# Block 0's gates by indirect accumulating DMAs into a zeroed table, in a hybrid decoder block on one Trainium2 core

## The chip, the cores and the metric

The kernel runs on one core of a Trainium2 chip, as one launch. The metric is the device time of that launch in microseconds (us). The core has five engines that work side by side, each with a queue of its own that it works off in order: TensorE (PE in the profile; its weight loads are the row PEld), VectorE (DVE), ScalarE (ACT), GpSimd (POOL) and SyncE (SP), which here issues the plain DMAs. Sixteen transfer engines move the data of all queues.

## The reference, cut to what matters

One decoder layer over 1024 tokens of width 1024. After a mixer (a gated DeltaNet and a sliding-window attention) comes PEER, a retrieval of single-neuron experts, and the change lies in it:

```
qry = (ht @ wq).reshape(T, 8, 2, 128)               # 8 heads, two half queries
sc = einsum("thpd,hpnd->thpn", qry, sub_keys)       # 128 scores per half
top_s, top_i = top_k(sc, 16)
cand = all sums of one score of each half           # 256 per head
best_s, best_pos = top_k(cand, 16)
expert = i1 * 128 + i2                              # of 16384 experts
gates = softmax(best_s)                             # 16 per head, 128 per token
act = gelu(x_token . u_tab[expert])
y_token = sum(gates * act * v_tab[expert])
```

A token so has 128 pairs (expert, gate). Within a head the 16 experts differ; two heads may pick the same expert, and then both gates count. After PEER come a gated projection and a last norm.

## The kernel before, in words

Tokens are handled in 8 blocks of 128. First comes the upstream part (`upstream`): the projections in two halves of 512 tokens (`project`, whose loop over 12 column tiles `ct` does the convolution), then, in four groups of two blocks, the mixers of the next group and the retrieval of this one (`retrieve`, which calls `topk` for each block). Weights and activations are split into two parts of type fp32r, so that one product becomes three matmuls (`mm3`, L141); other products are plain float32.

PEER's experts are evaluated in two ways. For blocks 5, 6 and 7 (`ABLK`), rows of the tables U and V are gathered by GpSimd, one indirect DMA of 128 rows for each of 128 pairs and each table, and VectorE multiplies and adds them (`gather_dots`, `gather_block`). For blocks 0 to 4 (`DBLK`, 640 tokens, `NU`) all 16384 experts are evaluated densely (`dense`, L924): in 128 chunks of 128 experts, U's product with the 640 tokens (in two `parts` of 320 columns, L938 to L940, 24 matmuls each), a gelu, a multiplication by the gates and a split into wh and wl; after each group of four chunks (`GC`) the product with V, 3 x 4 matmuls of 512 columns for each of 5 blocks and 2 halves.

The dense path needs the gates as a table over experts and tokens, with zeros where a token didn't pick an expert. `gbuild` (L837) makes it block by block: for four tokens at a time it compares a row of numbers with i1 and i2 (VectorE, tile `o12`, 128x1024), scales one of the two results by the gate (ScalarE, four times), multiplies the two on TensorE (float32, 128 columns, four products) and copies the result to `stage`; after 16 tokens `stage` goes to the DRAM table `gd` (1 MB). A block has 32 such steps and 8 writes. `dense` loads `gd` for a group of four chunks at a time into `Gt`, which has one buffer.

The order of the instructions of each engine is worked out ahead by a planner, from the order in which the program is written and a simulated time line; the calls `tick(us)` are in the program a count of VectorE work done, which a job may use to advance (before, none is there upstream). GpSimd does little upstream: the inverse roots of the norms and of the mixers (`rsqrt`, L154 to L157, tiles `rs_v`, `rs`, `rq`, `ro`) and small sets and copies.

Of the kernel before, what the change touches and what calls it, by code (L numbers as in the profile page):

```python
# [6 lines left out]

F32 = mybir.dt.float32
F32R = mybir.dt.float32r
# [9 lines left out]
P = 128  # L19
# [8 lines left out]
GROUPS = [[0, 1], [2, 3], [4, 5], [6, 7]]  # L28
HBLK = []
DBLK = [0, 1, 2, 3, 4]  # L30
ABLK = [5, 6, 7]
UBLK = HBLK + ABLK
BBLK = HBLK + DBLK
# [12 lines left out]
def _consts():  # L46
    import numpy as np

    r = np.arange(P)
    parts = [np.eye(P), r[:, None] <= r[None, :], r[:, None] > r[None, :], np.ones((P, P)),  # L50
             np.broadcast_to(r[None, :], (P, P)), r[None, :] > r[:, None]]
    for l in range(7):
        s = 1 << l
        same = (r[:, None] // (2 * s)) == (r[None, :] // (2 * s))
        low = same & (r[:, None] % (2 * s) >= s) & (r[None, :] % (2 * s) < s)
        parts.append(low if l == 0 else low.T[:, r % (2 * s) >= s])
    sel = np.zeros((P, 8 + 50 + 16 + 16 + 16))
    sel[:, :8] = (500000.0 ** (-np.arange(0, 16, 2) / 16)).astype(np.float32)
    widths = [16 // (a + 1) for a in range(16)]
    starts = np.concatenate([[0], np.cumsum(widths)[:-1]])  # L60
    sel[:, 58:74] = starts
    sel[:, 74:90] = np.concatenate([[0], np.diff(starts)])
    sel[:, 90:106] = np.arange(16)
    return np.concatenate([np.concatenate(parts, axis=1), sel], axis=1).astype(np.float32)
# [3 lines left out]
def block_kernel(ctx: ExitStack, tc, I, out, dbg=None):  # L68
# [6 lines left out]
    def copy(o, i, **k):  # L75
        return S.activation(o, i, AF.Copy, **k)  # L76

    def tt(o, a, b, op):
        return V.tensor_tensor(o, a, b, op)  # L79

    def stt(o, a, s, b, op0, op1, **k):
        return V.scalar_tensor_tensor(o, a, s, b, op0, op1, **k)  # L82

    def bc(ap, axis, n):
        u = ap.unsqueeze(axis)
        shape = list(u.shape)
        shape[axis] = n
        return u.to_broadcast(shape)
# [35 lines left out]
    UI, SL, ones = (C[n] for n in ("ui", "sl", "ones"))  # L124

    negt = c2.tile([P, 1], F32, name="negt")

    def load_consts():
        nc.sync.dma_start(ident, I["consts"][:, 0:P])
        nc.sync.dma_start(iota, I["consts"][:, 4 * P:5 * P])  # L130
        nc.sync.dma_start(cst, I["consts"][:, P:])
        V.tensor_copy(sel_b.rearrange("p s a h -> p (s a) h"), bc(sel[:, 58:106], 2, 8))
        V.memset(negt, NEG)

    def mm(o, l, r, start=True, stop=True):
        PE.matmul(o, l, r, start=start, stop=stop)  # L136
# [9 lines left out]
    x1d = dr.tile([NBLK, P, D], F32, name="x1d")  # L146
    h2d = dr.tile([len(UBLK), P, D], F32, name="h2d")
    h2Td = [dr.tile([P, DK, NU], F32, name=f"h2Td{i}") for i in range(2)]
    gd = dr.tile([NE // GC, P, NT // TB, GC, TB], F32, name="gd")

    eidx = cp.tile([P, len(UBLK), P], I32, name="eidx")
    gate_a = cp.tile([P, len(UBLK), P], F32, name="gate_a")

# [69 lines left out]
    def project(hf, es):  # L223
# [30 lines left out]
        for ct in range(12):  # L254
            wh, wl = weights(I["wc"][ct], [P, DK, P])
            if hf:
                for i in range(2 * ct, 2 * ct + 2):
                    cached_tile(i)
            raw = sm.tile([P, 3 + H], F32, tag="craw", name="craw")
            if hf:  # L260
                V.tensor_copy(raw[:, :3], prevs[:, ct])
            else:
                V.memset(raw[:, :3], 0.0)
            pc = bank("acc")
            for dk in range(DK):
                mm3(pc, wh[:, dk], wl[:, dk], hTh[:, dk], hTl[:, dk], dk == 0, dk == DK - 1)
            copy(raw[:, 3:], pc)
            if not hf:
                V.tensor_copy(prevs[:, ct], raw[:, H:H + 3])
            acc = sm.tile([P, H], F32, tag="cacc", name="cacc")  # L270
            copy(acc, raw[:, 3:], scale=convw[:, ct, 3:4])
            for j in (2, 1, 0):
                stt(acc, raw[:, j:j + H], convw[:, ct, j:j + 1], acc, ALU.mult, ALU.add)
            th = raw[:, 3:]
            S.activation(th, acc, AF.Tanh, scale=0.5)
            stt(acc, th, 1.0, acc, ALU.add, ALU.mult)
            qs = sm.tile([P, HB, P], F32, tag="cst", name="cst")
            pt = bank("tp", [HB, P])
            for i in range(HB):
                tr(pt[:, i, :], acc[:, i * P:(i + 1) * P])  # L280
            copy(qs, pt)
            nc.sync.dma_start(qkvn[b0:b0 + HB, :, ct, :].rearrange("b p c -> p b c"), qs)
# [474 lines left out]
    def topk(tk, bg, b, v, iu):  # L757
# [49 lines left out]
            summed(i2.rearrange("p (h k) -> p k h", h=8)[:, ks], t3)  # L807
            tick(7.5)

        ga = gate_a[:, UBLK.index(b)] if b in UBLK else flat[:, 2 * P:3 * P]  # L810
        gv = ga.rearrange("p (h k) -> p h k", k=16)
        tt(gv, bs, bs[:, :, 0:1].to_broadcast([P, 8, 16]), ALU.subtract)
        S.activation(gv, gv, AF.Exp)
# [3 lines left out]
        tt(gv, gv, bc(gs, 2, 16), ALU.mult)  # L817
        if b in UBLK:
            stt(eidx[:, UBLK.index(b)], i1, 128.0, i2, ALU.mult, ALU.add)
        if b in ABLK:  # L820
            return
        pt = bank("gm", [4, P])
        tr(pt[:, 0], i1)
# [9 lines left out]
            tick(1.4)  # L833

    slots = {}

    def gbuild(bg, b):  # L837
        tT = slots[b]
        for tb in range(P // TB):
            stage = bg.tile([P, NE, TB], F32, tag="stage", name="stage", bufs=2)  # L840
            for t0 in range(0, TB, 4):
                c0 = tb * TB + t0
                o12 = bg.tile([P, 2, 4, P], F32, tag="o12", name="o12", bufs=2)
                o1, o2 = o12[:, 0], o12[:, 1]
                tt(o12, bc(bc(iota, 1, 4), 1, 2), bc(tT[:, 0:2, c0:c0 + 4], 3, P), ALU.is_equal)
                for i in range(4):
                    copy(o2[:, i], o2[:, i], scale=tT[:, 2, c0 + i:c0 + i + 1])
                pg = bank("gm", [4, P])
                for i in range(4):
# [3 lines left out]
            nc.sync.dma_start(gd[:, :, BBLK.index(b) * (P // TB) + tb].rearrange("g p c t -> p g (c t)"),  # L853
                              stage.rearrange("p (g c) t -> p g (c t)", c=GC))

    def fetched(gp, tab, u, s):
# [59 lines left out]
        advance(1 << 20)  # L916

    def tick(us):
        credit[0] += us * RATE
        n = int(credit[0])  # L920
        credit[0] -= n
        advance(n)

    def dense(xB):  # L924
        with ExitStack() as es:
# [9 lines left out]
            for i in range(2):  # L935
                nc.sync.dma_start(hT[i].bitcast(F32), h2Td[i])
            nc.sync.dma_start(xB, x1d[BBLK[0]:BBLK[0] + NB].rearrange("b p d -> p b d"))
            nparts = (NU + 511) // 512  # L938
            width = (NU // nparts + TB - 1) // TB * TB
            parts = [(n0, min(width, NU - n0)) for n0 in range(0, NU, width)]  # L940
            total = len(ABLK) * 2 * P
            steps = NE + NE // GC * NB * 2
            count = [0, 0]
# [21 lines left out]

            nxt = prepared(0)
            for cg in range(NE // GC):
                Gt = ap.tile([P, NT // TB, GC, TB], F32, tag="Gt", name="Gt", bufs=1)
                nc.sync.dma_start(Gt, gd[cg])
                vs, ws = [], []  # L970
                for ci in range(GC):
                    c = cg * GC + ci
                    uh, ul, vh, vl = nxt
                    vs.append((vh, vl))
                    wh = ap.tile([P, NT], F32R, tag="wh", name="wh", bufs=GC + 1)
                    wl = ap.tile([P, NT], F32R, tag="wl", name="wl", bufs=GC + 1)
                    if NH:
                        gh = Gt[:, 0:NH // TB, ci, :]
                        sh = lambda x: x[:, 0:NH].rearrange("p (t k) -> p t k", k=TB)
                        copy(sh(wh), gh)  # L980
                        tt(sh(wl), gh, sh(wh), ALU.subtract)
                    for n0, n in parts:
                        pa = bank("u", [n])
                        for dk in range(DK):
                            mm3(pa, uh[:, dk], ul[:, dk], hT[0][:, dk, n0:n0 + n], hT[1][:, dk, n0:n0 + n],
                                dk == 0, dk == DK - 1)
                        ge = ap.tile([P, n], F32, tag="ge", name="ge")
                        S.activation(ge, pa, AF.Gelu_apprx_tanh)  # L988
                        g3 = ge.rearrange("p (t k) -> p t k", k=TB)
                        m0 = NH + n0  # L990
                        tt(g3, g3, Gt[:, m0 // TB:(m0 + n) // TB, ci, :], ALU.mult)
# [74 lines left out]
                post(*cur)  # L1066

    upstream()
    pools["gp"] = ctx.enter_context(tc.tile_pool(name="gp", bufs=GBUF, side="right", reuse_waits="tile"))
    pools["gx"] = ctx.enter_context(tc.tile_pool(name="gx", bufs=GXBUF, side="right", reuse_waits="tile"))  # L1070
    with tc.tile_pool(name="xB", bufs=1, side="right", reuse_waits="tile") as xp:
# [62 lines left out]
```

## Time and profile before

| what | us |
|---|---|
| median of 3 runs | 3038.61 (3036.75 to 3041.28) |
| the profiled execution, in all | 3043.6 |
| its span, from the first to the last instruction | 3041.8 |

The profile is of one execution. A row of the page or of a view names an engine, the line of the kernel, the operation, what it writes and what it reads; counts are behind an x; a busy time is the time in which the engine had something in it, and a matmul's length is from its dispatch to its modelled end, so that lengths of successive matmuls overlap.

### The profile page before, as it was taken

The numbers are of one execution on the slowest core, as the hardware profiler recorded it, in microseconds if no ns is written. First come the engines' busy times: TensorE is split into PE (matmuls) and PEld (weight loads), VectorE is DVE, ScalarE is ACT, GpSimd is POOL, SyncE is SP. The second block draws the span as 40 slices with busy tenths as digits, with TensorE's granted clock in tenths as the row PEclk, the third lists the DMA queues.
The fourth block names the chain that finished last, engine by engine and source line by source line (L and its number), as shares of the span: only waits on it lengthen the run. The fifth ranks groups of instructions, "written<-read, shape, count | busy, mean of one in ns | idle before, by whom it ended". The sixth has DMA issues, their size and how long they took to land. (4 is left out here: it accounts for less than half of the span.)

```text
span 3041.8 us, 49726 instructions
## 1 busy us (share of the span) xinstructions
PE 2936.2 (97%) x18287; PEld 2690.0 (88%) x18287; DVE 2499.4 (82%) x5023; ACT 1234.6 (41%) x2761; POOL 1068.4 (35%) x901
## 2 busy tenths in 40 slices
PE   7999999999999889999999999999999999999988
PEld 5887999999998789999999989998898898998967
DVE  5658636898999779988699889887998898899974
ACT  5556634488777663222222222232232232222223
POOL 0000000000000000765356556554656565556541
PEclk9989999999999999999999999999999999999989
DMA  7569657689889994999799989888999899899962
GB/s 236 142 223 364 206 191 248 215 223 243 237 242 270 287 279 141 351 338 348 272 342 354 330 319 369 329 332 300 335 351 345 318 358 332 306 337 347 324 256 89
DMA packets 449955, 869.30 MB, mean 286 GB/s; under 512 B 193456, under 2 KB 235824, under 8 KB 445360
## 3 DMA queue, kind: packets, MB, share of 16 engines
q1 hardware_dynamic: 339120, 463.43, 46.5%
q0 software_dynamic: 110592, 402.70, 36.4%
q8 instruction: 143, 2.34, 0.3%
q14 instruction: 100, 0.82, 0.1%
HBM read 766.40 MB, written 99.61 MB: 285 GB/s over the span
## 5 line engine op out<-in xcount | busy, mean ns | idle before, releaser
L136 PE MATMUL bk_u<-hT,uh 128*128 128x320 f32 x4096 | 915.4, 310 | 7.0 <-DMA hT<-h2Td 3.7
L136 PEld LDWEIGHTS bk_u<-hT,uh 128*128 128x128 f32 x4096 | 695.7, 189 | 23.2 <-ACT ge L988 4.6
L858 POOL DMA_INDIRECT rows<-in_u_dram,eidx x384 | 499.1, 1300 | 555.5 <-DVE dots L868 283.1
L136 PE MATMUL bk_u<-hT,ul 128*128 128x320 f32 x2048 | 635.0, 310 | 0.3 <-DVE ul L79 0.3
L858 POOL DMA_INDIRECT rows<-in_v_dram,eidx x384 | 498.6, 1298 | 350.1 <-DVE acc L82 287.5
L82 DVE SCALAR_TENSOR_TENSOR acc<-rows,dots,acc 128x1024 f32<-128x1024 f32 x384 | 492.2, 1282 | 35.4 <-DMA rows<-in_v_dram,eidx 24.5
L868 DVE CUSTOM_DVE_ANT_0 rows<-rows,h2n 128x1024 f32<-128x1024 f32 x384 | 459.9, 1223 | 27.5 <-DMA rows<-in_u_dram,eidx 27.3
L136 PEld LDWEIGHTS bk_u<-hT,ul 128*128 128x128 f32 x2048 | 386.5, 189 | 4.1 <-DVE ul L79 0.7
L988 ACT ACTIVATE ge<-bk_u 128x320 f32<-128x320 f32 x256 | 109.8, 431 | 603.3 <-PE bk_u L136 552.6
L136 PE MATMUL bk_y<-vh,wh 128*128 128x512 f32 x768 | 298.9, 391 | 3.0 <-DVE xB L79 3.0
L136 PE MATMUL bk_y<-vl,wh 128*128 128x512 f32 x768 | 299.9, 392 | 0.0
L136 PE MATMUL bk_y<-vh,wl 128*128 128x512 f32 x768 | 296.8, 393 | 2.6 <-DVE wl L79 2.6
L76 ACT ACTIVATE wh<-ge 128x320 fp32r<-128x320 f32 x256 | 118.7, 469 | 316.7 <-DVE ge L79 304.1
L76 ACT ACTIVATE o<-o,tT 128x128 f32<-128x128 f32 x640 | 204.5, 392 | 56.4 <-DVE o L79 55.1
L76 ACT ACTIVATE uh<-ur 128x1024 fp32r<-128x1024 f32 x128 | 135.3, 1057 | 226.4 <-PE bk_u L136 217.5
L136 PE MATMUL bk_gm<-o 128*128 128x128 f32 x1280 | 203.2, 286 | 22.5 <-ACT o L76 16.2
L136 PE MATMUL bk_s<-h,whi 128*128 128x256 f32 x1024 | 209.1, 295 | 3.3 <-DMA whi<-wqc 1.0
L79 DVE TENSOR_TENSOR o<-iota,tT 128x1024 f32<-128x1024 f32 x160 | 194.7, 1220 | 11.5 <-PE bk_gm L136 8.9
L136 PEld LDWEIGHTS bk_gm<-o 128*128 128x128 f32 x1280 | 178.2, 195 | 29.0 <-ACT o L76 20.2
L136 PE MATMUL bk_yp<-vl,wh 128*128 128x512 f32 x512 | 199.7, 391 | 0.0
L136 PE MATMUL bk_yp<-vh,wh 128*128 128x512 f32 x512 | 199.1, 391 | 0.0
L79 DVE TENSOR_TENSOR xB<-bk_y,xB 128x512 f32<-128x512 f32 x192 | 131.1, 689 | 79.5 <-PE bk_y L136 79.1
(302 smaller groups left out, 5840.5 us busy)
## 6 DMA issues: line engine op xcount, KB each, us to landing
ur<-in_uT_dram SPq DMA_DIRECT2D x128, 512.0 KB, 6.8
vr<-in_v_dram SPq DMA_DIRECT2D x128, 512.0 KB, 6.7
gd<-stage SPq DMA_DIRECT2D x40, 1024.0 KB, 7.3
Gt<-gd SPq DMA_DIRECT2D x32, 1280.0 KB, 9.6
wlo<-wqc SPq DMA_DIRECT2D x128, 256.0 KB, 4.6
whi<-wqc SPq DMA_DIRECT2D x128, 256.0 KB, 4.7
whi<-woc SPq DMA_DIRECT2D x64, 256.0 KB, 4.8
wlo<-woc SPq DMA_DIRECT2D x64, 256.0 KB, 4.7
```

The source lines that it names most:

```text
L76: return S.activation(o, i, AF.Copy, **k)
L79: return V.tensor_tensor(o, a, b, op)
L82: return V.scalar_tensor_tensor(o, a, s, b, op0, op1, **k)
L136: PE.matmul(o, l, r, start=start, stop=stop)
L858: G.indirect_dma_start(out=r, out_offset=None, in_=tab, in_offset=bass.IndirectOffsetOnAxis(ap=eidx[:, u, s:s + 1], axis=0))
L868: held_back(V.tensor_tensor_reduce(out=r, in0=r, in1=h2n, op0=ALU.mult, op1=ALU.add, scale=1.0, scalar=0.0, accum_out=dots[:, s:s + 1]))
L988: S.activation(ge, pa, AF.Gelu_apprx_tanh)
```

## The change

Block 0 (`SBLK`) gets a DRAM table of its own, `gsd`, one float per expert and token (8 MB). During the first half's projections eight DMAs of 1 MB write zeros into it. In `topk`, block 0 no longer transposes its indices and calls no `gbuild`; it computes for each pair the position in `gsd` (`sidx`) and keeps the gates in `sgate`. A generator, `scattered`, then issues 128 indirect DMAs on GpSimd's queue, each of which adds one gate per token to the table; those of a head wait until the 16 of the head before have landed. One is issued for each 2 us that `tick` counts (`SRATE` 0.5); each is placed by the planner behind the latest VectorE operation of `tt`, without a wait on it. `dense` takes its `parts` as 128 and 512 columns instead of 320 and 320, loads block 0's gates from `gsd` into a tile `Gs` and the rest from the smaller `gd`.

```diff
+            if not hf and 2 <= ct < 10:
+                zf = gsd.rearrange("(z p n k) o -> z p n (k o)", z=8, p=P, k=512)[ct - 2]
+                edge(nc.sync.dma_start(zf, bc(zero, 1, zf.shape[1])).ins, silu.ins.name, False)
...
-        if b in ABLK:
+        if b in SBLK:
+            si = SBLK.index(b)
+            stt(i1, i1, 128.0, i2, ALU.mult, ALU.add)
+            V.tensor_scalar(sidx[:, si], i1, float(NS), scol[:, si:si + 1], op0=ALU.mult, op1=ALU.add)
+            pools["sent"] = scattered(b)
+        if b in ABLK or b in SBLK:
             return
...
+    def scattered(b):
+        si = SBLK.index(b)
+        last = []
+        for h in range(8):
+            now = []
+            for k in range(16):
+                s = h * 16 + k
+                i = G.indirect_dma_start(
+                    out=lanes[16 * si + k], out_offset=bass.IndirectOffsetOnAxis(ap=sidx[:, si, s:s + 1], axis=0),
+                    in_=sgate[:, si, s:s + 1], in_offset=None, compute_op=ALU.add).ins
+                for j in last:
+                    edge(i, j, True)
+                if latest:
+                    edge(i, latest[0], False)
+                now.append(i.name)
+                yield
+            last = now
...
     def tick(us):
-        credit[0] += us * RATE
-        n = int(credit[0])
-        credit[0] -= n
-        advance(n)
+        job = pools.get("sent")
+        if job is None:
+            return
+        credit[0] += us * SRATE
+        while credit[0] >= 1:
+            credit[0] -= 1
+            next(job, None)
...
-            nparts = (NU + 511) // 512
-            width = (NU // nparts + TB - 1) // TB * TB
-            parts = [(n0, min(width, NU - n0)) for n0 in range(0, NU, width)]
+            parts = [(0, 128), (128, 512)]
...
+                Gs = ap.tile([P, GC, NS], F32, tag="Gs", name="Gs", bufs=1)
+                nc.sync.dma_start(Gs, gsd.rearrange("(g c p t) o -> g p c (t o)", c=GC, p=P, t=NS)[cg])
...
+                        if s0:
+                            tt(ge[:, 0:s0], ge[:, 0:s0], Gs[:, ci], ALU.mult)
+                        if n > s0:
+                            g3 = ge[:, s0:n].rearrange("p (t k) -> p t k", k=TB)
+                            r0 = (n0 + s0 - NS) // TB
+                            tt(g3, g3, Gt[:, r0:r0 + (n - s0) // TB, ci, :], ALU.mult)
```

## Rows read from the trace of the kernel before

**Rows 1.** The page's first part: the span, and each engine's busy time, share and instructions.
```profile
span 3041.8 us, 49726 instructions
PE 2936.2 (97%) x18287; PEld 2690.0 (88%) x18287; DVE 2499.4 (82%) x5023; ACT 1234.6 (41%) x2761; POOL 1068.4 (35%) x901
```

**Rows 2.** Stretches: length; busy us of PE, PEld, DVE, ACT, POOL; clock; DMA share; GB/s.
```profile
100.00:300.00 200.00, 188.44 (x1187) 166.75 (x1186) 131.56 (x240) 125.38 (x274) 8.41 (x15) 0.95 0.75 253
600.00:950.00 350.00, 341.84 (x2869) 331.57 (x2867) 328.43 (x1090) 275.02 (x827) 17.65 (x27) 1.00 0.87 240
950.00:1125.00 175.00, 149.27 (x1102) 143.56 (x1103) 149.91 (x494) 118.58 (x327) 2.55 (x4) 0.93 0.97 275
1125.00:2890.00 1765.00, 1753.52 (x9817) 1595.93 (x9816) 1548.28 (x2344) 475.30 (x772) 972.80 (x749) 1.00 0.89 325
```

**Rows 3.** Time line of TensorE in the dense stage: start us, length us, engine, line, operation.
```profile
2002.26 0.46 PE L136 MATMUL bk_u<-hT,uh 128*128 128x320 f32 x2
2002.55 0.31 PE L136 MATMUL bk_u<-hT,ul 128*128 128x320 f32 x1
2002.70 0.46 PE L136 MATMUL bk_u<-hT,uh 128*128 128x320 f32 x2
...
2004.51 0.39 PE L136 MATMUL bk_yp<-vh,wh 128*128 128x512 f32 x1
2004.74 0.39 PE L136 MATMUL bk_yp<-vl,wh 128*128 128x512 f32 x1
```

**Rows 4.** Groups by line and shape, TensorE's dense products: busy us, mean ns | idle before.
```profile
L136 PE MATMUL bk_u<-hT,uh 128*128 128x320 f32 x4096 | 915.4, 310 | 7.0 <-DMA hT<-h2Td 3.7 <-ACT ge L988 3.1
...
L136 PE MATMUL bk_y<-vl,wh 128*128 128x512 f32 x768 | 299.9, 392 | 0.0
...
L136 PE MATMUL bk_yp<-vl,wh 128*128 128x512 f32 x512 | 199.7, 391 | 0.0
```

**Rows 5.** Time lines of weight loads (PEld) and matmuls that nothing hides, upstream.
```profile
418.54 0.97 PEld L136 LDWEIGHTS bk_dn<-Y,A 128*128 128x128 f32 x8
...
418.65 1.00 PE L136 MATMUL bk_dn<-Y,A 128*128 128x64 f32 x8
419.49 0.33 PE L136 MATMUL bk_de<-B,cst 128*128 128x128 f32 x1
...
421.24 0.30 PEld L136 LDWEIGHTS bk_s<-whi,mT 128*128 128x128 f32 x2 [0.83 <-DMA whi<-woc]
```

**Rows 6.** The table builds of five blocks: groups by line, and TensorE's time line.
```profile
L79 DVE TENSOR_TENSOR o<-iota,tT 128x1024 f32<-128x1024 f32 x160 | 194.7, 1220 | 11.5 <-PE bk_gm L136 8.9
L76 ACT ACTIVATE o<-o,tT 128x128 f32<-128x128 f32 x640 | 204.5, 392 | 56.4 <-DVE o L79 55.1
L136 PE MATMUL bk_gm<-o 128*128 128x128 f32 x1280 | 203.2, 286 | 22.5 <-ACT o L76 16.2
...
700.49 0.60 PE L136 MATMUL bk_gm<-o 128*128 128x128 f32 x4
700.93 0.33 PE L136 MATMUL bk_dn<-Q,X 128*128 128x64 f32 x2
```

**Rows 7.** GpSimd: gathers and inverse roots; the longest waits; [idle before <-what ended it].
```profile
L858 POOL DMA_INDIRECT rows<-in_u_dram,eidx x384 | 499.1, 1300 | 555.5 <-DVE dots L868 283.1 <-PE bk_s L136 106.2 <-issue 64.9
...
1508.59 0.94 POOL L858 DMA_INDIRECT rows<-in_v_dram,eidx  x1 [0.30 <-DVE dots L79]
...
932.65 1.18 POOL L156 TENSOR_SCALAR rs_v<-so 128x4 f32<-128x4 f32 x1 [94.67 <-DVE o L79]
...
DVE h L82 <- POOL rs L157: 10.5, 2, 9.7
```

**Rows 8.** DMA issues: what, queue, kind, count, KB each, median us to landing.
```profile
gd<-stage SPq DMA_DIRECT2D x40, 1024.0 KB, 7.3
Gt<-gd SPq DMA_DIRECT2D x32, 1280.0 KB, 9.6
...
rows<-in_v_dram,eidx POOLq DMA_INDIRECT x384, 7.2
```

More of the change, by code (lines that the diff above doesn't have):

```diff
@@ L6 @@
 from concourse._compat import with_exitstack
+from concourse.ap import dram_disjoint_views
 F32 = mybir.dt.float32
@@ L30 @@
 DBLK = [0, 1, 2, 3, 4]
+SBLK = [0]
+NS = len(SBLK) * 128
+SRATE = 0.5
 ABLK = [5, 6, 7]
@@ L60, in _consts @@
     starts = np.concatenate([[0], np.cumsum(widths)[:-1]])
+    sel[:, 8] = r
     sel[:, 58:74] = starts
@@ L76, in copy @@
         return S.activation(o, i, AF.Copy, **k)
+    latest = []
     def tt(o, a, b, op):
-        return V.tensor_tensor(o, a, b, op)
+        i = V.tensor_tensor(o, a, b, op)
+        latest[:] = [i.ins.name]
+        return i
     def stt(o, a, s, b, op0, op1, **k):
@@ L126, in block_kernel @@
     negt = c2.tile([P, 1], F32, name="negt")
+    zero = c2.tile([P, 512], F32, name="zero")
+    scol = cp.tile([P, len(SBLK)], F32, name="scol")
     def load_consts():
@@ L133, in load_consts @@
         V.memset(negt, NEG)
+        V.memset(zero, 0.0)
+        for i in range(len(SBLK)):
+            V.tensor_scalar(scol[:, i:i + 1], sel[:, 8:9], float(i * P), None, op0=ALU.add)
     def mm(o, l, r, start=True, stop=True):
@@ L148, in block_kernel @@
     h2Td = [dr.tile([P, DK, NU], F32, name=f"h2Td{i}") for i in range(2)]
-    gd = dr.tile([NE // GC, P, NT // TB, GC, TB], F32, name="gd")
+    NO = NT - NS
+    gd = dr.tile([NE // GC, P, NO // TB, GC, TB], F32, name="gd")
+    gsd = dr.tile([NE * P * NS, 1], F32, name="gsd")
+    lanes = dram_disjoint_views(gsd, 16 * len(SBLK))
+    sidx = cp.tile([P, len(SBLK), P], I32, name="sidx")
+    sgate = cp.tile([P, len(SBLK), P], F32, name="sgate")
     eidx = cp.tile([P, len(UBLK), P], I32, name="eidx")
@@ L275, in project @@
             S.activation(th, acc, AF.Tanh, scale=0.5)
-            stt(acc, th, 1.0, acc, ALU.add, ALU.mult)
+            silu = stt(acc, th, 1.0, acc, ALU.add, ALU.mult)
+            if not hf and 2 <= ct < 10:
+                zf = gsd.rearrange("(z p n k) o -> z p n (k o)", z=8, p=P, k=512)[ct - 2]
+                edge(nc.sync.dma_start(zf, bc(zero, 1, zf.shape[1])).ins, silu.ins.name, False)
             qs = sm.tile([P, HB, P], F32, tag="cst", name="cst")
@@ L808, in topk @@
             tick(7.5)
-        ga = gate_a[:, UBLK.index(b)] if b in UBLK else flat[:, 2 * P:3 * P]
+        ga = gate_a[:, UBLK.index(b)] if b in UBLK else sgate[:, SBLK.index(b)] if b in SBLK else flat[:, 2 * P:3 * P]
         gv = ga.rearrange("p (h k) -> p h k", k=16)
@@ L835, in block_kernel, with edge @@
     slots = {}
+    def edge(a, b, sync):
+        tc.add_manual_dep(a, b, mybir.DependencyInfo(
+            mybir.DependencyClass.Sync if sync else mybir.DependencyClass.NoSync, mybir.DependencyReason.DATA),
+            reason="order of the gates")
+    def scattered(b):
[15 more added lines that the diff above has]
+            last = now
     def gbuild(bg, b):
@@ L852, in gbuild @@
                 yield
-            nc.sync.dma_start(gd[:, :, BBLK.index(b) * (P // TB) + tb].rearrange("g p c t -> p g (c t)"),
+            nc.sync.dma_start(gd[:, :, (BBLK.index(b) - len(SBLK)) * (P // TB) + tb].rearrange("g p c t -> p g (c t)"),
                               stage.rearrange("p (g c) t -> p g (c t)", c=GC))
@@ L967, in dense @@
             for cg in range(NE // GC):
-                Gt = ap.tile([P, NT // TB, GC, TB], F32, tag="Gt", name="Gt", bufs=1)
+                Gt = ap.tile([P, NO // TB, GC, TB], F32, tag="Gt", name="Gt", bufs=1)
                 nc.sync.dma_start(Gt, gd[cg])
+                Gs = ap.tile([P, GC, NS], F32, tag="Gs", name="Gs", bufs=1)
+                nc.sync.dma_start(Gs, gsd.rearrange("(g c p t) o -> g p c (t o)", c=GC, p=P, t=NS)[cg])
                 vs, ws = [], []
@@ L988, in dense @@
                         S.activation(ge, pa, AF.Gelu_apprx_tanh)
-                        g3 = ge.rearrange("p (t k) -> p t k", k=TB)
-                        m0 = NH + n0
-                        tt(g3, g3, Gt[:, m0 // TB:(m0 + n) // TB, ci, :], ALU.mult)
+                        m0 = n0
+                        s0 = max(0, NS - n0)
+                        if s0:
[4 more added lines that the diff above has]
+                            tt(g3, g3, Gt[:, r0:r0 + (n - s0) // TB, ci, :], ALU.mult)
                         copy(wh[:, m0:m0 + n], ge)
@@ L1068, in block_kernel @@
     upstream()
+    for _ in pools.pop("sent"):
+        pass
     pools["gp"] = ctx.enter_context(tc.tile_pool(name="gp", bufs=GBUF, side="right", reuse_waits="tile"))
```

## The prediction

> **What bounds the kernel now.** I read the first part of the page, then the stages, then single instructions. TensorE is busy 97% of the span, VectorE 82%, GpSimd 35% [rows 1]; as matmul ends are modelled, that only says where to look. By stages [rows 2] the kernel is two kernels. From 1125 to 2890 us (the dense stage) TensorE is busy 1753.5 of 1765 us and VectorE 1548. From 600 to 950 us, where the tables of gates are built beside the mixers and the retrieval, TensorE has 342 and VectorE 328 of 350 us; from 950 to 1125 both fall to about 150 of 175.
>
> Is TensorE really the dense bound? There I take starts, not lengths, because a matmul's row (0.31 or 0.39 us) is a latency. Three 320-column products start at 2002.26, two in one row, then 2002.55, and the next three at 2002.70: 0.44 us for three, 0.147 each. 512-column ones start at 2004.51 and 2004.74: 0.23 [rows 3]. The counts over 128 chunks are 6144 products for U (the row of 4096 is that of two of the three parts) and 3 x (768 + 512) for V [rows 4], that is 48 and 30 per chunk: 48 x 0.147 + 30 x 0.23 = 13.96 us, and 127 chunks make 1773 us against the stage's 1765. So the dense stage is a gapless stream of matmuls, and a nanosecond more per matmul is paid in full.
>
> **The change, part by part.**
>
> *The split of U's columns.* The diff's smallest line falls on that stream: 320 + 320 columns become 128 + 512. Each chunk keeps 48 products and 640 columns, so by columns alone nothing would change: from 512 to 320 columns the spacing falls by 0.083 us per 192, so 128 would take 0.147 - 0.083 = 0.064, and 0.064 + 0.23 equals 2 x 0.147. But each product has its own weight load, and no row before has a split-precision (fp32r) product under 256 columns. The nearest rows are loads that nothing hides. Eight loads for 64-column float32 products take 0.97 us, of which the last is 0.19: 0.78/7 = 0.111 us each, and their eight matmuls go from 418.65 to 419.49, 0.105 each, though they stream the fewest columns of all. A load of split-precision weights after 0.83 us of idle time is followed by the next 0.30 - 0.19 = 0.11 us later [rows 5]. So a load of 128 columns costs 0.11 us whatever the type, hidden under the matmul before it where that streams longer. 320 columns hide it; 128 don't. Nor does it help that longer matmuls stand between: in the run of eight no load starts before the matmul ahead of it, so behind a short one a load is always bare. I take 0.111 for each 128-column product: 24 x (0.111 + 0.23 - 0.294) = 1.13 us per chunk, x 128 = **+144 us**. The ends are 0.064 (load hidden after all, 0 us) and the float32 product of 128 columns, which runs as two matmuls (1280 for 640 scaled blocks) of 0.11 (four from 700.49 to 700.93, [rows 6]), 0.22 in all: 24 x 0.156 x 128 = +479 us. The value is nearest to the load rows because the type's loads themselves stand there.
>
> The Trainium skill ("TensorE: Matmul & The Clock Gate", section "Back-to-back issue gap") gives about 81 ns for a sustained pair of load and 128-column matmul, below this trace's 0.111; by it the term would be an estimated 24 x 0.017 x 128 = +52 us, which is a rival below. Its figure for 512 columns, 131 ns, disagrees with this trace's 0.23 us, so I trust the rows.
>
> *Block 0's table build goes.* Of five equal builds one is dropped: 32 of 160 comparisons at 1.220 us on VectorE (39 us), 128 of 640 scalings and 32 copies on ScalarE, 256 of 1280 matmuls on TensorE at 0.11 (28 us) [rows 6]. It lies in the stretch from 600 us, where both engines are over 93% busy. TensorE has the fuller row there, so 28 us are what it gives back; 39 if VectorE turns out to be the bound, 0 if the chain of dependent steps is (from 950 us it seems to be: both engines idle). I take **-28**. ScalarE, at 275 of 350 us, isn't what is late next; the other engine is.
>
> *128 scatters on GpSimd.* No accumulating scatter is in the trace; the nearest row is the gather, 1.30 us mean, 0.94 when undisturbed, plus 0.30 between two [rows 7]. So 128 x 1.24 to 1.6 = 159 to 205 us of GpSimd, which in that stretch has 18 of 350 us of work. By the ticks (0.5 per credited us, 256 us of credits: what is left of group 0, the two mixers of group 2, group 1's retrieval) they end within block 3's build, around 950 us: one per 2.7 us. What queues behind a scatter is an inverse root: eight pairs from 608 to 960 us, the last at 932.65, each with a VectorE step waiting; before, such a wait cost 9.7 us once [rows 7]. With GpSimd half taken, a pair meets a running scatter half the time and waits half of it: 8 x 0.5 x 0.7 = 3 us. Each head's first scatter waits until the 16 before it have landed; a gather lands after 7.2 us [rows 8], so GpSimd stalls about 7.2 - 2.7 = 4.5 us seven times, a tenth of the stretch, another 3 us. I take **+6**, between 0 (TensorE has other work queued) and 70 (every pair waits out a scatter and a landing, 8 x 8.8). The Trainium skill's "DMA: Bandwidth & Descriptors", section "Anatomy of one DMA", has some 2.0 us fixed for such a transfer; by it an estimated 3 us of this term would go. The rows have no small one to show.
>
> *Zeroing the table.* Eight writes of 1 MB on SP's queue among the first half's projection weights. A 1 MB write lands in 7.3 us [rows 8]; the transfer engines are 75% busy from 100 to 300 us [rows 2]. Each weight load behind one comes up to 7 us late, but three buffers lie ahead: **+3**, between 0 and 58. In return eight table writes of the same size are gone from the stretch at 87%; the scatters' 128 x 128 four-byte elements come instead. I set this at nothing, hidden by what was freed; if they cost more, the retrieval's weights are late.
>
> *Small things at nothing.* The index arithmetic, the zero tile and 256 KB per group as their own load (Gt shrinks by as much): VectorE has 12% room in the dense stage and keeps its counts (one multiply and one subtract per part, the same 640 columns), and the extra load is issued with Gt, which the stream of V products covers. If that cover failed, each of the 32 groups would wait for up to one landing of 9.6 us [rows 8].
>
> **The sum**: 144 - 28 + 6 + 3 = +125 us. The profiled execution took 3043.6 us in all (its span is 3041.8, [rows 1]) and would take 3168.6; the median of the runs is 3038.61, 5 below, so I predict 3164. Its own range: dense +130 to +155 (spacings 0.11 and 0.227 to 0.232), build -39 to 0, GpSimd 0 to 40, zeroing 0 to 15, not all at one end: +70 to +185, 3108 to 3224.
>
> **The rivals.**
>
> *The load is hidden.* Against my term: if TensorE could hold two loads ahead, a short matmul among 512-column ones would hide its successor's load, the dense stage would stay, and the sum is -28 + 9 = -19: 3020; with all of VectorE's 39 us 3008. For it: between 320 and 512 columns the spacing follows the columns alone. Against it: the 64-column rows, where eight in a row never beat the load. It decides from a mean spacing of the 128-column products under 0.064 + 19/3072 = 0.070 us. Chance 0.06.
>
> *Half hidden.* If a load could begin while the matmul ahead still waits, the spacing would lie between the ends, at the middle 0.088: 24 x 0.024 x 128 = +74, less 19, 3094. For it: a load's row is 0.19 long, more than the 0.147 between two starts, so part of its length lies beside its own matmul [rows 3, 5]. Against it: no row shows a spacing between. Chance 0.04. The Trainium skill's figure above would make it an estimated 3072.
>
> *Narrow split-precision products run as float32*, two passes instead of one. For it: no row of the type under 256 columns. Against it: it is the same instruction with a shorter operand. 479 - 19 = +460: 3499. Chance 0.10.
>
> *The scatters don't spread.* GpSimd runs in order, and an inverse root there waited 94.67 us for its input [rows 7]; scatters queued behind such a wait come in a burst, and the next root stands behind them, or the last ones land late and the first table load waits. Half of the scatters in two bursts is 2 x 32 x 1.24 = 79 us on the path: 125 + 79 - 6, 3237. For it: VectorE's and TensorE's order is fixed around those roots. Against it: each scatter is placed behind a VectorE step of its own time. Chance 0.05.
>
> My case keeps 0.75. The range 3105 to 3240 holds it and the burst; the float32 case is left out above and the two hidden cases below, together 0.20. This kernel's runs lie within 0.2%, 6 us, so 3038.6 +/- 6 is no change: faster 0.06 and same 0.01, from the hidden load alone; slower 0.93.
>
> **What would show it.** In the changed profile: U's products in two forms, 128 and 512 columns, 3072 each; starts of the 128-column ones 0.11 us apart, their loads back to back; the dense stage near 1910 us instead of 1765. 32 comparisons fewer and the first dense chunk's end about 20 us earlier. GpSimd with some 170 us more before 1000 us and no VectorE wait on an inverse root over 10 us. I am wrong if the 128-column starts lie 0.07 us apart or less, if each product shows as two matmuls, or if the dense stage begins later than now.

## The result and the profile after

The changed kernel takes 3234.05 us (median of 4 runs, 3221.86 to 3240.92) against 3039.95 (3036.75 to 3042.76) for the kernel before on the same chip: a ratio of 1.0646, 95% interval [1.063, 1.0661]. It is slower by 194 us, where 125 were forecast; the time lies in the range of 3105 to 3240, but 70 us above the time predicted, 10 above what my own case could reach (3224), and 3 us from the price of the burst, a rival with a chance of 0.05. So the sum has to be taken apart. The profiled execution took 3221.86 us, 178.3 more than that of before. It is the shortest of its four, so the trace explains 178 us and not all 194.

The page's first part, which answers to [rows 1]:

```profile
span 3220.0 us, 49339 instructions
...
PE 3073.8 (95%) x18028; PEld 2682.4 (83%) x18028; DVE 2482.9 (77%) x4995; ACT 1176.7 (37%) x2600; POOL 1336.7 (42%) x1029
```

GpSimd has 268 us more. The same stretches as [rows 2], the dense one at its new length:

```profile
100.00:300.00 200.00, 189.39 (x1206) 167.84 (x1205) 134.79 (x246) 127.53 (x278) 8.82 (x16) 0.96 0.82 280
600.00:950.00 350.00, 299.35 (x2430) 288.67 (x2430) 276.17 (x940) 216.26 (x660) 219.75 (x146) 0.93 0.84 191
950.00:1125.00 175.00, 145.23 (x1051) 136.87 (x1049) 147.98 (x479) 116.21 (x317) 12.50 (x10) 0.93 0.99 268
1125.00:3080.00 1955.00, 1941.32 (x10040) 1641.98 (x10041) 1589.71 (x2466) 475.00 (x783) 1039.48 (x759) 1.00 0.85 300
```

Two things stand out. The dense stage is as gapless as before and longer. And from 600 to 950 us TensorE has lost 42 us of work and VectorE 52; dropping one table build takes only 28 (256 matmuls at 0.11 us) and 39. Work was pushed out of this stretch. Three marks of TensorE's time line split the 178 us; they are the first and the last start in these groups, two of before and two of after:

```profile
L136 PE MATMUL bk_y<-vh,wh x768: 388/388/505, 1142.7 to 2919.5; 128*128 128x512 f32 x192
L136 PE MATMUL bk_y<-vh,wl x768: 388/394/502, 1151.5 to 2920.0; 128*128 128x512 f32 x192
L150 PE MATMUL bk_y<-vh,wh x768: 391/396/628, 1174.3 to 3104.5; 128*128 128x512 f32 x192
L150 PE MATMUL bk_y<-vh,wl x768: 392/396/398, 1182.2 to 3105.0; 128*128 128x512 f32 x192
```

| mark | before | after | difference |
|---|---|---|---|
| first V product into `bk_y` | 1142.7 | 1174.3 | +31.6 |
| from it to the last V product | 1777.3 | 1930.7 | +153.4 |
| from there to the end of the span | 121.8 | 115.0 | -6.8 |

*The dense stage.* TensorE's time line, as [rows 3] (start, length, operation):

```profile
2002.06 0.27 PE L150 MATMUL bk_u<-hT,ul 128*128 128x128 f32 x1
2002.17 0.39 PE L150 MATMUL bk_u<-hT,uh 128*128 128x128 f32 x2
2002.39 0.27 PE L150 MATMUL bk_u<-hT,ul 128*128 128x128 f32 x1
...
2004.41 0.27 PE L150 MATMUL bk_u<-hT,ul 128*128 128x128 f32 x1
...
2005.04 0.40 PE L150 MATMUL bk_u<-hT,ul 128*128 128x512 f32 x1
...
2007.79 0.39 PE L150 MATMUL bk_u<-hT,ul 128*128 128x512 f32 x1
...
2008.71 0.39 PE L150 MATMUL bk_y<-vl,wh 128*128 128x512 f32 x1
...
2011.28 0.39 PE L150 MATMUL bk_y<-vh,wh 128*128 128x512 f32 x1
```

Three 128-column products start every 0.33 to 0.34 us, and the 21 from 2002.06 to 2004.41 take 2.35 us: 0.112 each. Twelve 512-column ones from 2005.04 to 2007.79 take 2.75: 0.229 each. The weight loads of the 128-column ones run at the same pace as these, 0.11 between two:

```profile
2002.11 0.30 PEld L150 LDWEIGHTS bk_u<-hT,uh 128*128 128x128 f32 x2
2002.34 0.19 PEld L150 LDWEIGHTS bk_u<-hT,ul 128*128 128x128 f32 x1
2002.45 0.30 PEld L150 LDWEIGHTS bk_u<-hT,uh 128*128 128x128 f32 x2
```

Eleven V products, from 2008.71 to 2011.28, take 2.57 us, 0.234 each. In the kernel before ten take 2.29, 0.229 each:

```profile
2006.11 0.39 PE L136 MATMUL bk_y<-vh,wh 128*128 128x512 f32 x1
...
2008.40 0.39 PE L136 MATMUL bk_yp<-vh,wh 128*128 128x512 f32 x1
```

Over all such pairs of the two traces the median went from 229 to 234 ns.

*The stretch ahead of it.* Two roots are the clue. At the last root `rq` the kernel was 22 us ahead of before (714.9 against 737.0), at the next root `rs`, that of group 2's retrieval, it was 28 behind (833.0 against 805.4). Between and behind them, the stretches:

```profile
750.00:800.00 50.00, 45.05 (x340) 40.81 (x339) 48.01 (x225) 19.13 (x55) 40.79 (x25) 0.97 0.80 189
800.00:850.00 50.00, 12.31 (x72) 11.03 (x72) 13.55 (x26) 14.51 (x44) 39.44 (x28) 0.66 0.51 73
850.00:900.00 50.00, 47.32 (x373) 45.40 (x373) 43.43 (x101) 33.04 (x101) 38.58 (x24) 0.93 0.92 198
```

From 800 to 850 us TensorE, VectorE and ScalarE do a quarter to a third of their work and the transfers move 73 GB/s; only GpSimd goes on. TensorE, which idles there, has a mean granted clock of 0.66, between its two levels (columns as in [rows 2]). The longest waits from 800 to 900 us say for whom, and GpSimd's time line what it was doing:

```profile
PE bk_s L153 <- DVE h L91: 32.1, 1, 32.1
DVE h L91 <- POOL rs L176: 31.9, 1, 31.9
DVE zs L91 <- POOL ro L176: 6.8, 1, 6.8
```
```profile
706.24 0.51 POOL L175 TENSOR_SCALAR rs_v<-so 128x4 f32<-128x4 f32 x1 [22.81 <-ACT junk L682]
...
829.30 1.54 POOL L876 DMA_INDIRECT gsd<-sgate,sidx  x1 [0.30 <-issue]
831.15 1.54 POOL L876 DMA_INDIRECT gsd<-sgate,sidx  x1 [0.30 <-issue]
832.76 0.19 POOL L175 TENSOR_SCALAR rs_v<-ss 128x1 f32<-128x1 f32 x1
833.03 0.58 POOL L176 TENSOR_TENSOR rs<-rs_v,mhalf 128x1 f32<-128x1 f32 x1
```

54 scatters run almost back to back from 717 to 832 us, most of them 1.54 us and 0.30 to the next. A root of 0.8 us stands behind them, VectorE waits 31.9 us for it, and TensorE for VectorE. (The lines ahead of the root are alike back to 803.5, one every 1.85 us.)

### The profile page after: what moved, and what is told of

The parts are those of the page before. It is cut to its first block, busy times and chain, and to the rows that moved or that the text cites. A ratio compares the mean times of both kernels' runs of the same rounds, so it can differ in the third digit from the quotient of the medians.

```text
span 3220.0 us, 49339 instructions
## 1 busy us (share of the span) xinstructions
PE 3073.8 (95%) x18028; PEld 2682.4 (83%) x18028; DVE 2482.9 (77%) x4995; ACT 1176.7 (37%) x2600; POOL 1336.7 (42%) x1029
## 4 chain that ended last, share of the span: by engine, by line
PE 79%; DVE 7%; DMA 5%; POOL 4%; issue 3%; ACT 2%; SPq 0%; POOLq 0%; ACTq 0%; DVEq 0%
PE bk_u L150 30%; PE bk_y L150 16%; PE bk_yp L150 11%; PE bk_acc L150 7%; PE bk_s L150 7%; POOL gsd L876 3%; PE bk_dn L150 2%; PE bk_gm L150 2%; PE bk_g L150 1%; DVE o L86 1%; PE bk_sw L150 1%; DVE get L86 1%; PE bk_dn L153 1%; DMA prd<-pr 1%; PE bk_tp L153 1%
## 5 line engine op out<-in xcount | busy, mean ns | idle before, releaser
L150 PE MATMUL bk_u<-hT,uh 128*128 128x128 f32 (+1 forms) x4096 | 986.5, 332 | 1.5 <-DMA hT<-h2Td 0.8
L909 POOL DMA_INDIRECT rows<-in_u_dram,eidx x384 | 533.8, 1390 | 578.2 <-DVE dots L919 229.8
L150 PE MATMUL bk_u<-hT,ul 128*128 128x128 f32 (+1 forms) x2048 | 681.7, 333 | 1.6 <-DVE ul L86 1.6
L1042 ACT ACTIVATE ge<-bk_u 128x128 f32<-128x128 f32 (+1 forms) x256 | 107.7, 426 | 459.4 <-PE bk_u L150 391.5
L876 POOL DMA_INDIRECT gsd<-sgate,sidx x128 | 216.4, 1691 | 67.8 <-issue 36.1
L81 ACT ACTIVATE vh<-vr 128x1024 fp32r<-128x1024 f32 x128 | 132.5, 1058 | 290.7 <-PE bk_y L150 151.3
L86 DVE TENSOR_TENSOR ul<-ur,uh 128x1024 fp32r<-128x1024 f32 x128 | 156.2, 1220 | 93.1 <-ACT uh L81 91.9
L81 ACT ACTIVATE wh<-ge 128x512 fp32r<-128x512 f32 (+1 forms) x256 | 114.8, 466 | 296.4 <-DVE ge L86 282.5
L86 DVE TENSOR_TENSOR vl<-vr,vh 128x1024 fp32r<-128x1024 f32 x128 | 156.1, 1220 | 73.7 <-ACT vh L81 73.5
L150 PE MATMUL bk_yp<-vh,wl 128*128 128x512 f32 x512 | 193.4, 398 | 0.0
```

What stands on the lines that cost most here:

```text
L86: i = V.tensor_tensor(o, a, b, op)
L876: i = G.indirect_dma_start(out=lanes[16 * si + k], out_offset=bass.IndirectOffsetOnAxis(ap=sidx[:, si, s:s + 1], axis=0), in_=sgate[:, si, ...
L909: G.indirect_dma_start(out=r, out_offset=None, in_=tab, in_offset=bass.IndirectOffsetOnAxis(ap=eidx[:, u, s:s + 1], axis=0))
```

## The experiments

There were two leading theories. One is the prediction's own: the split costs what a bare load of 0.11 us costs, in the dense stage alone. The other comes from the trace after: the burst ahead of group 2's root costs some 40 to 54 us. Against the first stood a fixed penalty per narrow matmul, against the second that the scatters' traffic delays the weights. Every ratio is to the kernel before on the same chip.

**The changed kernel with the old split.**

```diff
-            parts = [(0, 128), (128, 512)]
+            parts = [(0, 320), (320, 320)]
```

> The changed kernel with U's columns split 320 + 320 again. Bare-load theory (128-column products are paced at 0.11 us by their weight load): 24 x (0.111 + 0.23 - 0.294) x 128 = 144 us go, 3234 to about 3090, and the dense stage is back at about 1775 us from the first V product to the last. If V's products are also slower only because of the narrow split (0.234 us between starts instead of 0.229), another 19 us go: 3071. Rival, the dense stage is longer for another reason (the second table load, the gathers started later): 3200 or more.

Measured: 3091.92 us (3086.68 to 3096.47), ratio 1.0182 [1.0161, 1.0203]. The changed kernel without its narrow products loses 142 us of its 194. What is left, 56 us, is all the rest of the change, forecast as -19.

**The kernel before with the new split alone.**

```diff
-            parts = [(n0, min(width, NU - n0)) for n0 in range(0, NU, width)]
+            parts = [(0, 128), (128, 512)]
```

> The kernel before with nothing changed but U's columns, 128 + 512. Bare-load theory: +144 us on 3040, 3184, 128-column starts 0.11 us apart; with V's products at 0.234 us too, 3203. Rival, the split costs only beside the scatters and the second table: within 20 us of 3040.

Measured: 3191.23 (3185.65 to 3195.01), 1.0507 [1.0489, 1.0525]: +155 us. By these two the split is worth 142 to 155 us, against +144. The traces are closer: from the first V product to the last this kernel takes 1922.3 us, 145.0 more than before, and the changed kernel takes 144.7 more than the one with the old split (1930.7 against 1786.0). The V products of this kernel stand 230 ns apart, so it is not the split that slows them in the changed one.

**The kernel before split in 192 and 448 columns** (one run).

```diff
+            parts = [(0, 192), (192, 448)]
```

> The kernel before with U's columns split 192 + 448. Bare-load theory (a matmul shorter than its successor's weight load is paced by that load): 192 columns stream in 0.147 - 128 x 0.083/192 = 0.092 us, so their starts still lie 0.111 apart, and 448 columns take 0.203: 24 x (0.111 + 0.203 - 0.294) x 128 = +61 us, about 3100. Rival, a narrow product carries a fixed penalty whatever its width: 0.111 - 0.064 = 0.047 more than its columns, starts 0.139 apart, +147 us, 3185.

Measured: 3106.33. Its time line in the dense stage:

```profile
2012.74 0.28 PE L136 MATMUL bk_u<-hT,ul 128*128 128x192 f32 x1
...
2014.42 0.27 PE L136 MATMUL bk_u<-hT,ul 128*128 128x192 f32 x1
...
2015.30 0.36 PE L136 MATMUL bk_u<-hT,ul 128*128 128x448 f32 x1
...
2017.12 0.36 PE L136 MATMUL bk_u<-hT,ul 128*128 128x448 f32 x1
```

Fifteen 192-column products take 1.68 us, 0.112 each, the same as 128-column ones although they stream half as much again; nine 448-column ones take 1.82, 0.202 each. Per chunk 24 x (0.112 + 0.202 - 0.294) = 0.48, x 128 = +61 us, with 3106 - 3036 = 70 measured. A fixed penalty of 0.047 us per narrow matmul would have put the starts 0.139 us apart and the run at 3185. It falls; a floor at the load's pace stands.

**The changed kernel without its 128 scatters** (block 0's experts are left out).

```diff
-            pools["sent"] = scattered(b)
...
-    for _ in pools.pop("sent"):
-        pass
```

> The changed kernel without its 128 scatters: the table stays zero, so block 0's experts are left out. Theory that the scatters on GpSimd hold up an inverse root (VectorE waited 31.9 us for one): the first V product starts at about 1120 instead of 1174 us, as the 22 us that the dropped table build gave until 737 us are kept, and the time is 3234 - 54 = 3180. Rival, the planner's other order or the zero writes cost it: the first V product stays at 1160 or later and the time at 3220 or more.

Measured: 3175.64 (3174.85 to 3181.57), 1.0468 [1.045, 1.0486], 58 us less than with them (54 by the ratios). The stall is gone: from 800 to 850 us TensorE has 47 us where it had 12.

```profile
800.00:850.00 50.00, 47.41 (x405) 46.84 (x406) 48.75 (x122) 35.98 (x112) 1.21 (x2) 1.00 0.84 214
```

But the first V product comes at 1128.9, only 14 us before that of the kernel before, while the last table step comes 41 us before it (1070 against 1111). The relief of the build so arrives on VectorE and not at the dense stage. The chain of waits from 1050 to 1130 us has these among its longest pieces (start, length, what):

```profile
1074.08 5.47 DMA wlo<-wqc
1079.60 7.47 PE bk_s L150 x46
1088.14 4.17 DMA wlo<-wqc
```

The query products of group 3's retrieval there wait for their weights. That the transfers are what keeps back the other 27 us is read from this chain and not tested by a run.

**The old split and slower scatters.**

```diff
+            parts = [(0, 320), (320, 320)]
-SRATE = 0.5
+SRATE = 0.35
```

> 320 + 320 columns, and the scatters at 0.35 per credited us instead of 0.5, so spread over about 366 credited us instead of 256. GpSimd-queue theory (a scatter takes 1.85 us with its gap, and at 0.5 they stood back to back from 716 to 831 us): no VectorE wait on a root over 8 us, the first V product at 1120 to 1135 us, 40 us under the run with 320 + 320 columns alone: 3030 to 3050. Rival, the scatters' memory traffic costs the time and not their place in the queue: the same time as with 320 + 320 columns alone, within 10 us.

Measured: 3055.28 (3052.57 to 3057.28), 1.0063 [1.0046, 1.008]: 37 us less than with the faster rate, with the same number of scatters. The two views that showed the stall:

```profile
800.00:850.00 50.00, 45.59 (x363) 44.51 (x364) 48.46 (x131) 39.32 (x123) 39.73 (x23) 0.93 0.97 225
```
```profile
DVE h L91 <- POOL rs L176: 4.6, 3, 3.0
```

GpSimd is as busy there as in the changed kernel (39.7 us of 50), and VectorE's longest wait for a root is 3.0 us instead of 31.9. Counted in the two traces, 26 scatters stand ahead of the root `rq` at the faster rate and 27 at this one, but 54 and 32 between it and group 2's root `rs`. So not the load on GpSimd costs the time but its order, and not the traffic, which is the same in sum. The time is a little above the range that I had given, and 19 us above before.

**The same rate with the new split.**

```diff
-SRATE = 0.5
+SRATE = 0.35
```

> The changed kernel with its split of 128 and 512 columns, but one scatter issued per 2.9 us of ticks (SRATE 0.35) instead of per 2.0. If the burst of scatters ahead of group 2's root costs what e1 against e5 showed (37 us), and what the split costs comes in the dense stage alone, this gives 3234 - 37 = 3197 us (3185 to 3205), with the longest VectorE wait on a root at 3 us. If the two add up otherwise (the dense stage hides or repeats a part of what comes before it), it differs from that by more than 12 us.

Measured: 3188.58 (3184.43 to 3191.29), 1.0507 [1.0489, 1.0524]. The burst costs 45 us here, by ratios 1.4% or 42 us, and 37 with the old split. The first V product comes at 1137.0, 37 us before that of the changed kernel, and VectorE's longest wait for a root is 3.0 us again. The two costs add up as expected.

**Where the last 19 us are.** The old split with slower scatters still lost to before. Its V products stood 234 ns apart, and the tiles `wh`, `uh` and `hT` lie 1056 bytes further in SBUF than before, as the new constants stand ahead of them (worked out from the sizes in the program, 512 + 512 + 32; no trace shows an address). Three kernels shift them with unused bytes among the constants: the kernel before by 32 (8 floats), and the one with the old split and slower scatters by 96 and by 64 more (24 and 16 floats), which puts the tiles 1152 and 1120 bytes from their places before.

```diff
+    cp.tile([P, 8], F32, name="pad")
```

> The kernel before with 32 unused bytes per partition among the constants and nothing else, which moves uh, ul, hT, wh and wl from 32 to 64 bytes past a multiple of 128. Place theory: V's products 0.234 us apart and +19 us, 3055. Rival: 0.229 and 3037, no change.

Measured: 3045.69 (3041.13 to 3056.99), 1.0037 [1.0022, 1.0051]. 32 unused bytes cost the kernel before 10 us, and its V products' median spacing went from 229 to 234 ns (the trace is of the slowest of its eight runs). Ten intervals take 2.33 us here:

```profile
2027.12 0.39 PE L137 MATMUL bk_y<-vh,wh 128*128 128x512 f32 x1
...
2029.45 0.40 PE L137 MATMUL bk_y<-vl,wh 128*128 128x512 f32 x1
```

So the place matters, by half of what I had expected.

> 320 + 320 columns, scatters at 0.35, and 96 unused bytes per partition among the constants, which puts U's and the scaled gates' tiles (uh, ul, hT, wh, wl) back at 32 bytes past a multiple of 128, as in the kernel before; without them they lie at 64. Theory that this place makes V's products slower (0.234 us between starts instead of 0.229): 0.229 again, 3840 x 0.005 = 19 us less, 3055 to about 3036. Rival, the second table or the later gathers slow them: 0.234 and 3055 as without.

Measured: 3059.76 (3049.95 to 3064.91), 1.0073 [1.0047, 1.0099]; spacing 233 ns.

> As the run with 96 unused bytes, but with 64, so that the same tiles lie at a multiple of 128. Place theory in its simplest form (an even place is good, 64 is bad): 0.229 or less and 3036 or less. Rival: the place has nothing to do with it, 0.234 and 3055.

Measured: 3055.23 (3052.97 to 3056.73), 1.0066 [1.0046, 1.0087]; spacing 232 ns. A rule modulo 128 bytes fell with these two.

**The old split and slower scatters, shifted by 2048 bytes against the kernel before.**

```diff
+    cp.tile([P, 248], F32, name="pad")
```

> e5_slow_scatter with 992 unused bytes per partition between the constants, so that wh comes to lie 2048 bytes above its place in the kernel before. If what shifts the V products' spacing from 229 to 234 ns is the place of their operands modulo a power of two up to 2048, the median spacing is back at 229 ns, which over 3840 products is 19 us less than e5: about 3037, level with the kernel before. If it is not the place modulo such a power (another rule, or other tiles), the spacing stays at 232 to 234 ns and the time at about 3055.

Measured: 3047.18 (3040.56 to 3054.68), 1.0035 [1.002, 1.0049]. The V products of the kernel with 1120 bytes and, below, of this one:

```profile
2004.49 0.40 PE L151 MATMUL bk_yp<-vh,wl 128*128 128x512 f32 x1
...
2007.06 0.40 PE L151 MATMUL bk_y<-vh,wl 128*128 128x512 f32 x1
```
```profile
1999.63 0.39 PE L151 MATMUL bk_yp<-vh,wh 128*128 128x512 f32 x1
...
2001.91 0.39 PE L151 MATMUL bk_y<-vh,wl 128*128 128x512 f32 x1
```

Eleven intervals of the first take 2.57 us, 0.234 each; ten of the second 2.28, 0.228. The spacing of before is back, and with it 8 us. That a shift of 2048 bytes leaves the spacing as it was and 32, 1056, 1120 and 1152 do not is shown; which tile of the three it is, and whether there is a period (it would be over 128 and divide 2048), is not. The rest of the forecast (level with before) did not come: the last V product is 4.7 us earlier than that of before, but the end is 130 us after it instead of 122. Every changed kernel with the old split has such a tail, of 127 to 131 us, and the kernel before with 32 bytes has 121.

**One multiplication by the gates again** (on the kernel shifted by 2048 bytes). In the old split the part with both tables takes two on VectorE. Block 0's table gets the order of `Gt`, so that one does.

```diff
-                            tt(ge[:, 0:s0], ge[:, 0:s0], Gs[:, ci], ALU.mult)
...
+                        tt(g3, g3, Gt[:, n0 // TB:(n0 + n) // TB, ci, :], ALU.mult)
```

> e12_pad_992 with the table of block 0 laid out as Gt is (the position of a pair is worked out with the chunk innermost but one), so that it lands in rows of the same tile and each part of 320 columns takes one multiplication by the gates on VectorE again, as before, in place of two for the part that held both tables: 128 fewer. e12's last V product came 4.7 us earlier than that of the kernel before, and its end 3.2 us later, with 12 us more of VectorE work in the dense stage. If that work delays the gathered blocks and so the tail, the tail goes from 130 back to some 122 us: 3039 (3034 to 3044). If the tail is longer for another reason, it stays at 3047.

Measured: 3049.87 (3047.38 to 3054.05), 1.0043 [1.0031, 1.0055]. VectorE's work from 1125 to 2890 us fell by 16 us (1560.7 to 1544.6), and the tail did not: 131 us. The theory fell. What the traces show near the tail is the last accumulations of the gathered blocks, here in the kernel before, the one shifted by 2048 bytes and this one (count, shortest, median and longest ns, first and last start):

```profile
L82 DVE SCALAR_TENSOR_TENSOR acc<-rows,dots,acc x5: 1279/1282/1285, 2929.0 to 2938.5; 128x1024 f32<-128x1024 f32 x5
```
```profile
L91 DVE SCALAR_TENSOR_TENSOR acc<-rows,dots,acc x5: 1277/1279/1280, 2933.9 to 2948.8; 128x1024 f32<-128x1024 f32 x5
```
```profile
L91 DVE SCALAR_TENSOR_TENSOR acc<-rows,dots,acc x11: 1276/1280/1285, 2934.2 to 2963.3; 128x1024 f32<-128x1024 f32 x11
```

They end 10 and 25 us later than before, but the tails of the two are alike, so the accumulations alone do not set it. In the kernel shifted by 2048 bytes ScalarE then waits 18.7 us for the load of `xt`, the last gathered block, a wait that is not among those of before. Why the accumulations come late, and what lengthens the tail, is open.

**Slower still** (on the kernel with one multiplication).

```diff
-SRATE = 0.35
+SRATE = 0.3
```

> e13_one_multiply with one scatter per 3.3 us of ticks (SRATE 0.3). Without any scatter the first V product came at 1128.9, in e12 at 1140.9 and before at 1142.7. If scatters that run beside the mixers and the root of group 3 still cost a part of these 12 us, thinning them gives 2 to 8 us less than e13. If the limit of that stretch is the transfers of the weights, nothing changes (within 2 us), and if the last scatters now stand before the first load of the gates, it is 3 us or more longer.

Measured: 3059.45 (3056.73 to 3066.21), 1.0078 [1.0065, 1.0092], 9.6 us more than at 0.35. The time agrees with the last of the three forecasts, the place does not: the loss is there before 810 us, at the same root as in the changed kernel. Its wait from 720 to 825 us, and GpSimd's time line:

```profile
DVE h L91 <- POOL rs L177: 16.2, 1, 16.2
```
```profile
801.33 1.54 POOL L881 DMA_INDIRECT gsd<-sgate,sidx  x1 [2.21 <-DMA gsd<-sgate,sidx]
802.93 0.19 POOL L176 TENSOR_SCALAR rs_v<-ss 128x1 f32<-128x1 f32 x1
803.41 1.58 POOL L881 DMA_INDIRECT gsd<-sgate,sidx  x1 [0.28 <-issue]
805.29 1.56 POOL L881 DMA_INDIRECT gsd<-sgate,sidx  x1 [0.30 <-issue]
806.30 1.17 POOL L177 TENSOR_TENSOR rs<-rs_v,mhalf 128x1 f32<-128x1 f32 x1
```

Scatters stand ahead of the root and even between its two steps. Fewer of them per us did not thin this place: 35 stand between `rq` and `rs` here, and 30 at the faster rate of 0.35. The rate of 0.35 was a lucky order and not a safe one. No kernel of these beats the kernel before. The roots were not tried on another engine.

## Why the prediction was right, and where it was not

**The bound (right).** The gapless stream of matmuls in the dense stage was the right thing to read: the two split experiments move the time by what the spacings say, with the rest of the kernel unchanged or changed.

**The split, +144 (right).** Spacings of 0.111 to 0.112 and 0.229 in place of twice 0.147 make 24 x (0.111 + 0.229 - 0.294) x 128 = 141 us by this trace; the two experiments give 142 and 155 us by their times, and 145 us each from the first V product to the last. The bare load of [rows 5] was the right nearest row. The hidden, the half-hidden and the float32 rivals fell: the median over 2886 pairs of 128-column products is 0.111 us, and each is one matmul (3072 of either form). In one place the first rival has a point. Behind a 512-column product the second of a run starts 0.06 us after the first, all 170 times; from the third on it is 0.11. The Trainium skill ("TensorE: Matmul & The Clock Gate", section "LDWEIGHTS (loading the stationary operand)") gives a load's time as its columns divided by 1.2, some 107 ns for 128; the trace's 0.111 agrees. The 192-column run shows that it is a floor.

**The V products (missed).** The sum has no term for them: it kept their spacing at the 0.23 of before. The median went from 229 to 234 ns, which over 3840 products would be an estimated 19 us; the stage shows about half of that. Without the narrow split the changed kernel takes 8.7 us more than before from the first V product to the last (1786.0 against 1777.3), and the kernel before with 32 unused bytes 11.1 more (1788.4). 144.7 and 8.7 are the 153.4 measured. The cause is where the tiles lie, which neither the diff nor a row of before shows.

**The table build, -28 (right in size, given back).** At `rq` before the burst the kernel was 22 us ahead, with the zeroing's 4 us gain in it. But without a scatter only 14 us are left at the first V product. I had read the idle engines from 950 us [rows 2] as a chain and put its 0 among the bounds; that was the better half of the answer.

**GpSimd, +6 (wrong).** This is the step that failed. The first V product comes 45 us later with the scatters than without (1174.3 against 1128.9), 37 later than at a rate of 0.35, and the medians with and without differ by 58, or 54 by the ratios. The price of one scatter was too low: 1.24 to 1.6 us with its gap were forecast, and it is 1.85 undisturbed and 1.99 in the mean (1.69 and 0.30). The landing was as forecast: 7 waits for the head before, 29.9 us in all, against 7 x 4.5; in the run with the old split and slower scatters one lands after 6.3 us in the median, near the gather's 7.2. What failed most was "a pair meets a running scatter half the time and waits half of it". That averages over a queue that is taken evenly. A tie behind a VectorE step says only that a scatter is not earlier than that step; nothing says that it is not later. At the forecast's one per 2.7 us from the first at 597.7 us on, an estimated 44 would have been out when the burst began at 716.7, and 26 were; in between GpSimd had idled 22.8 us for a root's input and 12.5 us for TensorE. The 54 that follow take 2.1 us each, ahead of the next root in the queue. At 0.35 nearly as many (27) stand ahead of `rq` and only 32 between it and `rs`. That the backlog comes from GpSimd's waits is argued from these counts; that the root stands behind it is shown. This is the rival "the scatters don't spread", priced at 3237 and given 0.05. [Rows 7] had its sign, a root that waits 94.67 us for its input, and I set it aside because each scatter has a step of its own. By the traces the sum is 144.7 (split) + 8.7 (the dense stage otherwise) - 13.9 (all ahead of it, without scatters) + 45.4 (scatters) - 6.8 (tail) = 178 us. The range held only because it reached to that rival, and that its 3237 is 3 us off is luck: it priced two bursts at 79 us on top of a build that gave 28 back, and there was one, of 45, with 14 given back.

**The zeroing, +3 (about nothing).** The last product of the projections (`bk_acc`) starts 4.4 us earlier than before (411.9 against 416.3) though the transfers' share from 100 to 300 us rose from 0.75 to 0.82.

**The small things at nothing (right).** VectorE in the dense stage has 1590 of 1955 us, and the instructions that read `Gs` waited for ScalarE (2.4 us in all) and never for its load. The tail even came out 7 us shorter, with the last accumulation starting 5.6 us behind the last V product instead of 18.5; the kernel before with 128 and 512 columns has a tail of 117 us, too, and its last accumulation at 7.1. That the gathers have room in a longer dense stage fits this.

**The signs named.** Two forms at 0.11, a longer dense stage and 32 comparisons fewer came. "The first dense chunk's end about 20 us earlier" and "no VectorE wait on an inverse root over 10 us" did not, and the dense stage begins later than before, which I had named as what would prove me wrong. It does, for the upstream part. GpSimd has 213 us more before 1000 us (265.8 against 53.0), not some 170: the scatters' price again.

## What to carry to other kernels

A stream of matmuls with a weight load each had the load's pace as its floor, 0.11 us here: before columns are moved between two parts, see that each part streams longer than that; 192 columns cost here what 128 do. An instruction tied behind another engine's work is kept from being early, not from being late: on an in-order queue, count what can be held up at once ahead of each short instruction that others wait for, and not a mean share. When two kernels differ by under half a per cent, shift their tiles to the same places before looking for a reason in the schedule.

## What the runs showed of the hardware

- An accumulating indirect DMA of 128 four-byte elements takes GpSimd 1.54 us when undisturbed (mean 1.69) and 0.30 to the next, where the gather of 128 rows of 4 KB took 0.94 and 0.30 [rows 7]. The smaller transfer was the dearer one to issue; whether adding or scattering makes it so, no run shows.
- 128- and 192-column split-precision products both start 0.112 us apart, 448-column ones 0.202 and 512-column ones 0.229; the second of a run behind a 512-column product comes 0.06 us after the first.
- The place of SBUF tiles is worth 2% of a 512-column product: 229 or 234 ns, and 10 us of this kernel for 32 unused bytes; a shift by 2048 bytes leaves the spacing at 229.
